# A new order table and one more product on constant tiles, in a decoder block whose instructions a planner puts in order

## The chip, the cores and the metric

One core of one Trainium2 chip. The metric is the time that the device takes for one execution, in microseconds; lower is better. The core's engines are named as in the profile: PE is TensorE (matrix products), PEld its loading of the stationary operand, DVE is VectorE, ACT is ScalarE, POOL is GpSimd, and SP is SyncE, whose queue here issues every transfer. PSUM is the memory that PE writes its results to.

## The reference, cut to what matters

A decoder block on 256 rows of 1024 numbers, in float32. Three mixers work on the normalised rows and are added with gates; then follows a gated channel mixer.

```python
h = rmsnorm(x, g_pre_mix)
z = h @ w_in
q_nsa, kv_nsa, g_nsa, qkv_ml, if_ml, o_ml, q_mem, g_merge = split(z)
...            # compressed, selected and windowed attention
y_nsa = gb[..., 0:1] * o_cmp + gb[..., 1:2] * o_slc + gb[..., 2:3] * o_win
...            # chunkwise mLSTM with a causal convolution of width 4
y_ml = sigmoid(o_ml) * h_ml
y_mem = memory_xattn(q_mem, mem, g_mem, w_mem_kv)   # keys and values: rmsnorm(mem) @ w_mem_kv
gm = sigmoid(g_merge)
y = gm[0] * (y_nsa @ w_proj_nsa) + gm[1] * (y_ml @ w_proj_ml) + gm[2] * (y_mem @ w_proj_mem)
x = x + rmsnorm(y @ w_out, g_post_mix)
h = rmsnorm(x, g_pre_ffn)
gu = h @ w_ffn_in
gate, up = gu[..., :2816], gu[..., 2816:]
x = x + rmsnorm((silu(gate) * up) @ w_ffn_down, g_post_ffn)
```

## The kernel before, in words

**The products.** Each large product is made of three products on rounded parts: an operand is split into a high part and a low part (`split`: ACT writes the high part `hi`, DVE subtracts it from the source and writes the low part `lo`), and PE adds high by high, high by low and low by high in PSUM. The weights come as 161 units of 128x1024 float32 (512 KB each). `fetch` issues the transfer of a unit into a tile `raw` on SP's queue; there are four buffers of `raw`. `parts` splits it into `whi` and `wlo` (four buffers each; for the first product of the feed-forward the parts are called `wq`). So a weight unit goes through SP, ACT, DVE and PE in that order, and each `raw` buffer comes free when its split is done.

**The stages.** First the keys and values of the memory tokens are made: `memt` holds the first inputs, `mh` and `ml` are the high and low parts of the memory tokens, and the results are in tiles `pd` and `pss` (PSUM tiles in general are called `pd`, `pss`, `ptn`, `pvn`, `sc`, `psm`, and so on). `mem_v` is the second of these products; its units are `whi`, `wlo` with `mh`, `ml`. Meanwhile the rows `x` are normalised (`xn`, `xt`, `rbc`) and split into `hh`; the memory's row norms come from `mn`. Then come the projections of `w_in`; four groups of attention in two halves each (`nsa_half`: `sc` is the scores on keys `kk` and queries `qs`, `mx` the masked maximum, `pp` and `pc` the exponentials, `ptn`, `pTh`, `pTl` their transposes and parts, `pvn` the product with the values, `ylo` and `yT` its sum), with the mLSTM's tasks put between the halves (`cx`, `cy` is the convolution, `vml` the values); then the merge. `w_out` is a product to two row halves of 128 rows (`tb` = 0, 1), each in two halves of 512 columns. Behind it `scaled` gives `xg` (the rows that go into the feed-forward), PE transposes `xg` into a PSUM tile that the trace calls `ptx`, and `split` writes it to `xc`, the operand of all of the feed-forward. The output of `ffn_down` goes out in pieces: per row half, columns 0 to 512, 512 to 768 and 768 to 1024 of a tile that the trace calls `z`, each one DVE instruction and one transfer.

**The order.** The kernel doesn't call engines directly. `Plan` records every operation with what it depends on; `schedule` then puts them in order with a list scheduler that keeps its own clock for every engine: of the operations that are ready on an engine it takes the one with the lowest `urge`. The urge is a rank, found by `choose` in some passes over the recorded operations, less a number from the table `EARLY` (operation's number: nanoseconds; a positive number makes the operation earlier). `lay_out` gives tiles their place, and `issue` emits the operations in that order; since it is one helper that calls the engines, all instructions of the kernel have the line L622 in the profile, and one goes by the tiles' names. All products, all splits and all transfers are in the hands of this order; each engine carries out its own instructions strictly one after the other, so an instruction that waits holds up those behind it on its engine.

**The start.** `warm_up(n)` records n products of a 128x128 tile of ones with itself into a PSUM tile `warm` that nobody reads. They stand in front of the first real product, and need no transfer. The table's numbers count recorded operations, so each product more in front moves the numbers of all later operations by one.

Of the kernel before, what the change touches and what calls it, by code (L numbers as in the profile page):

```python
# [167 lines left out]
class Plan:  # L168
# [363 lines left out]
    MATMUL, SLACK, PASSES = (-3.0, 0.0), (60.0, 130.0), 3  # L532

    EARLY = """
# [15 lines left out]
    """  # L550

    def choose(self):
# [73 lines left out]
def block_kernel(ctx, tc, order, xN, xT, memN, head, cst, vec, row, wg, w1, w2, W, out):  # L626
# [38 lines left out]
    def ps_v(shape, name="pv"):  # L665
        return psum.tile(shape, F32, tag="v", bufs=1, name=name)
# [95 lines left out]
    def warm_up(n):  # L762

        ps = ps_v([P, P], "warm")
        for _ in range(n):
            PE.matmul(ps, ones, ones, start=True, stop=True)
# [50 lines left out]
    part(1544, 2056)  # L817
    fetch(("mem_k", 2))
    part(2056, 3080)
    warm_up(8)  # L820
    warm = one.tile([P, 1], F32, name="warm")
    ACT.activation(warm, ones[:, 0:1], AF.Copy)
    kps = [ps_d([P, 2, S]) for _ in range(2)]
# [750 lines left out]
```

## Time and profile before

| | |
|---|---|
| runs | 524.69, 524.74, 526.28 us; median 524.74 |
| the profiled execution | 526.83 us; its span is 525.0 us, the granted clock 0.998 |
| PE busy | 516.7 us of the span, 3516 instructions in the profile |
| DVE, ACT, POOL busy | 412.9, 354.0, 6.2 us |
| transfers | 97.69 MB, 186 GB/s in the mean |

A row of the timeline reads: start in us, duration in us, engine, line, operation, output tile <- input tiles, shape, and how many instructions of one kind it groups (x4); in brackets the idle time of the engine ahead of it and what ended that. "SPq" is the issue of a transfer, not its flight. A product of float32 operands (`ones`) stands as two records. A row of windows gives, for a stretch from:to, its length and each engine's busy time with the number of instructions, then clock, share of the transfer engines and GB/s.

### The profile page before, as it was taken

The numbers are of one execution on the slowest core, as the hardware profiler recorded it, in microseconds if no ns is written. First come the engines' busy times: TensorE is split into PE (matmuls) and PEld (weight loads), VectorE is DVE, ScalarE is ACT, GpSimd is POOL, SyncE is SP. The second block draws the span as 40 slices with busy tenths as digits, with TensorE's granted clock in tenths as the row PEclk, the third lists the DMA queues.
The fourth block names the chain that finished last, engine by engine and source line by source line (L and its number), as shares of the span: only waits on it lengthen the run. The fifth ranks groups of instructions, "written<-read, shape, count | busy, mean of one in ns | idle before, by whom it ended". The sixth has DMA issues, their size and how long they took to land.

```text
span 525.0 us, 9545 instructions
## 1 busy us (share of the span) xinstructions
PE 516.7 (98%) x3516; PEld 475.6 (91%) x3516; DVE 412.9 (79%) x865; ACT 354.0 (67%) x724; POOL 6.2 (1%) x19
## 2 busy tenths in 40 slices
PE   8999999999999999999999999999999999999995
PEld 8999998989899999999999998788888888888884
DVE  5699898798989998988887888956776787664543
ACT  7777997577799887978995446554655665564531
POOL 0000000000000100000000000000000000000000
PEclk9999999999999999999999999999999999999999
DMA  8986546635343273264464766545555565566512
GB/s 316 416 310 265 182 140 209 214 122 199 122 152 131 86 275 122 85 199 161 162 201 160 215 223 213 193 131 190 180 187 194 186 201 184 196 196 199 187 61 81
DMA packets 28703, 97.69 MB, mean 186 GB/s; under 512 B 3312, under 2 KB 5232, under 8 KB 28400
## 3 DMA queue, kind: packets, MB, share of 16 engines
q1 hardware_dynamic: 28656, 97.07, 55.5%
q8 instruction: 28, 0.46, 0.3%
q14 instruction: 19, 0.16, 0.1%
HBM read 94.96 MB, written 1.05 MB: 183 GB/s over the span
## 4 chain that ended last, share of the span: by engine, by line
PE 91%; DMA 4%; DVE 3%; issue 1%; ACT 1%; DVEq 0%; ACTq 0%
PE pd L622 49%; PE pss L622 30%; PE pvn L622 2%; PE sc L622 2%; PE ptn L622 2%; DMA raw<-in_W 2%; DMA gp<-in_row 1%; DVE wlo L622 1%; DMA memt<-in_head 1%; PE ph L622 1%; DVE mrg L622 1%; PE psm L622 1%; PE pvm L622 1%; PE ptx L622 1%; PE pq L622 0%
## 5 line engine op out<-in xcount | busy, mean ns | idle before, releaser
L622 DVE TENSOR_TENSOR wlo<-raw,whi 128x1024 fp32r<-128x1024 f32 (+1 forms) x159 | 191.0, 1209 | 67.8 <-ACT whi L622 66.7
L622 ACT ACTIVATE whi<-raw 128x1024 fp32r<-128x1024 f32 (+1 forms) x159 | 165.9, 1052 | 110.1 <-PE pd L622 49.8
L622 PE MATMUL pd<-hh,whi 128*128 128x256 f32 x800 | 146.8, 280 | 0.0
L622 PEld LDWEIGHTS pd<-hh,whi 128*128 128x128 f32 x800 | 123.5, 188 | 0.2
L622 PE MATMUL pd<-hh,wlo 128*128 128x256 f32 x400 | 111.8, 280 | 0.0
L622 PEld LDWEIGHTS pd<-hh,wlo 128*128 128x128 f32 x400 | 75.2, 188 | 0.1
L622 PE MATMUL pss<-xc,whi 128*128 128x512 f32 x168 | 43.4, 393 | 0.0
L622 PE MATMUL pss<-whi,u 128*128 128x512 f32 x132 | 42.0, 390 | 0.0
L622 PEld LDWEIGHTS pss<-xc,whi 128*128 128x128 f32 x168 | 30.6, 188 | 5.3
L622 DVE CUSTOM_DVE_ANT_0 sc<-sc,msk 128x16 f32<-128x16 f32 (+2 forms) x96 | 27.3, 317 | 5.8 <-PE sc L622 3.7
L622 PE MATMUL pd<-xc,whi 128*128 128x512 f32 x120 | 31.8, 393 | 0.0
L622 PE MATMUL pd<-whi,hh 128*128 128x512 f32 x96 | 31.6, 397 | 0.0
L622 PEld LDWEIGHTS pss<-whi,u 128*128 128x128 f32 x132 | 24.8, 188 | 5.2
L622 ACT ACTIVATE pp<-sc,mx 128x128 f32<-128x128 f32 (+1 forms) x64 | 26.8, 434 | 0.5 <-DVE mx L622 0.3
L622 PE MATMUL pss<-wlo,u 128*128 128x512 f32 x66 | 25.7, 390 | 0.0
L622 PEld LDWEIGHTS pd<-xc,whi 128*128 128x128 f32 x120 | 22.2, 188 | 3.8
L622 PEld LDWEIGHTS pss<-xc,wlo 128*128 128x128 f32 x168 | 22.2, 188 | 1.7
L622 PE MATMUL pss<-xc,wlo 128*128 128x256 f32 x168 | 22.5, 278 | 0.0
L622 PEld LDWEIGHTS pd<-whi,hh 128*128 128x128 f32 x96 | 17.9, 188 | 3.2
L622 PE MATMUL pd<-wlo,hh 128*128 128x512 f32 x48 | 19.1, 397 | 0.0
L622 PE MATMUL sc<-kk,qs 128*128 128x272 f32 (+1 forms) x96 | 18.2, 291 | 0.0
L622 PEld LDWEIGHTS pd<-xc,wlo 128*128 128x128 f32 x120 | 15.8, 188 | 1.2
(328 smaller groups left out, 1040.4 us busy)
## 6 DMA issues: line engine op xcount, KB each, us to landing
raw<-in_W SPq DMA_DIRECT2D x161, 512.0 KB, 4.0
w<-in_w SPq DMA_DIRECT2D x2, 1024.0 KB, 7.9
xn<-in_xN SPq DMA_DIRECT2D x2, 512.0 KB, 9.1
mn<-in_memN SPq DMA_DIRECT2D x2, 512.0 KB, 7.9
xt<-in_xT SPq DMA_DIRECT2D x2, 512.0 KB, 8.7
kk<-kk SPq DMA_DIRECT2D x8, 128.0 KB, 3.2
x<-in_xN SPq DMA_DIRECT2D x2, 512.0 KB, 4.5
memt<-in_head SPq DMA_DIRECT2D x1, 512.0 KB, 7.4
```

What stands on the lines that cost most here:

```text
L622: op.ins_ = getattr(op.real, op.method)(*map(arg, op.a), **{k: arg(x) for k, x in op.kw.items()})
```

## The change

Two things. The table `EARLY` is replaced by another, with other operations and other numbers. And `warm_up(8)` becomes `warm_up(9)`.

```diff
     EARLY = """
-    2:182343850 3:30107850 4:28731400 5:28733050 6:1189450 7:1191000 145:12450 149:-600 151:1850 152:5000
...
-    4295:4700 4296:5700 4665:-6000 4673:-8200 5055:24850 5056:4350 5057:31850
+    2:267862150 3:43604600 4:40989750 5:40991450 6:1891200 50:2941700 146:9450 149:-2200 150:-1600 153:3350
...
+    4665:-550 5056:50900
     """
...
-    warm_up(8)
+    warm_up(9)
```

The computed operations stay the same, but for the one product. The order moves on every engine, in hundreds of places. Three of them follow, each as the engine's rows before and after; the numbers in names count tiles, and those of the two kernels don't match each other.

First ACT around the end of `w_out`, at about 331 to 336 us of the profile before. `whi_4597`, `whi_4615` and `whi_4636` (after: `whi_4602`, `whi_4625`, `whi_4644`) are splits of weight units, `xc` is the split of the transposed rows (of two tiles `ptx1`, which the trace calls `ptx`), `sq` a sum of squares. Before:

```order
L622 ACTIVATE wq_4585<-raw_4546 128x1024 [waits DMAHW2_49]
L622 ACTIVATE whi_4597<-raw_4566 128x1024 [waits DMAHW3_49,DVE_49,PE_49]
L622 ACTIVATE whi_4615<-raw_4581 128x1024 [waits DMAHW4_49,DVE_49,PE_49]
L622 ACTIVATE xc_4626<-ptx1_4609 128x4x128 [waits PE_49]
L622 ACTIVATE xc_4626<-ptx1_4618 128x4x128 [waits PE_49]
L622 ACTIVATE whi_4636<-raw_4599 128x1024 [waits DMAHW5_49,DVE_49]
L622 ACTIVATE sq_4643,ss_4521<-pd_4574 128x512 [waits PE_49,Activation_49]
```

And after:

```order
L622 ACTIVATE wq_4585<-raw_4555 128x1024 [waits DMAHW2_49]
L622 ACTIVATE whi_4602<-raw_4571 128x1024 [waits DMAHW3_49,DVE_49,PE_49]
L622 ACTIVATE xc_4619<-ptx1_4610 128x4x128 [waits PE_49]
L622 ACTIVATE whi_4625<-raw_4588 128x1024 [waits DMAHW4_49,DVE_49]
L622 ACTIVATE xc_4619<-ptx1_4617 128x4x128 [waits PE_49]
L622 ACTIVATE sq_4641,ss_4517<-pd_4575 128x512 [waits PE_49,Activation_49]
L622 ACTIVATE whi_4644<-raw_4605 128x1024 [waits DMAHW5_49,DVE_49]
```

The first `xc` now stands ahead of the second `whi`; the second `xc` stays behind it.

Second ACT at about 114 to 127 us, in the attention's second group. `ylo` ends one half of the group, `pp` and `pc` are exponentials of the next half's scores `sc`, `vml` the mLSTM's values. Before:

```order
L622 ACTIVATE ylo_1643<-pvn_1587 64x512 [waits PE_49]
L622 ACTIVATE whi_1655<-raw_1450 128x1024 [waits DMAHW4_49,PE_49]
L622 ACTIVATE whi_1669<-raw_1504 128x1024 [waits DMAHW5_49,PE_49]
L622 ACTIVATE vml_869<-pd_1552 128x4x128 [waits PE_49]
L622 ACTIVATE whi_1683<-raw_1572 128x1024 [waits DMAHW6_49,PE_49]
L622 ACTIVATE vml_869<-pd_1639 128x4x128 [waits PE_49]
L622 ACTIVATE whi_1706<-raw_1616 128x1024 [waits DMAHW7_49,Activation_49]
L622 ACTIVATE whi_1744<-raw_1685 128x1024 [waits DMAHW0_49,DVE_49,PE_49]
L622 ACTIVATE pp_1758,sm_1757<-sc_1695,mx_1738 128x256 [waits DVE_49]
```

And after:

```order
L622 ACTIVATE ylo_1645<-pvn_1587 64x512 [waits PE_49]
L622 ACTIVATE pc_1654,sm_1653<-sc_1627,mx_1638 128x16 [waits DVE_49]
L622 ACTIVATE pp_1658,sm_1653<-sc_1627,mx_1638 128x256
L622 ACTIVATE whi_1666<-raw_1451 128x1024 [waits DMAHW4_49,PE_49]
L622 ACTIVATE whi_1679<-raw_1504 128x1024 [waits DMAHW5_49,PE_49]
L622 ACTIVATE vml_803<-pd_1554 128x4x128 [waits PE_49]
L622 ACTIVATE whi_1698<-raw_1594 128x1024 [waits DMAHW6_49,PE_49,Activation_49]
L622 ACTIVATE vml_803<-pd_1648 128x4x128 [waits PE_49]
L622 ACTIVATE whi_1720<-raw_1629 128x1024 [waits DMAHW7_49,Activation_49]
L622 ACTIVATE whi_1753<-raw_1692 128x1024 [waits DMAHW0_49,DVE_49,PE_49]
L622 ACTIVATE pp_1658,sm_1653<-sc_1632,mx_1638 128x256 [waits DVE_49]
```

One pair of exponentials has moved from behind five `whi` and two `vml` to the place right behind `ylo`. PE makes the scores that they read ahead of it (three `sc` products among those of the first `pd` that `vml` reads), and one later `sc` product needs the exponential to be done.

Third DVE at the end. Before:

```order
L622 SCALAR_TENSOR_TENSOR z_6072<-z_6072,ss,x_2576 128x256 x2
L622 SCALAR_TENSOR_TENSOR z_6072<-pd,rf,go 128x512
L622 RECIPROCAL ss<-ss 128x1
L622 SCALAR_TENSOR_TENSOR z_6072<-z_6072,ss,x_2576 128x256 x2
L622 SCALAR_TENSOR_TENSOR z_6072<-z_6072,ss,x_2576 128x512
```

And after:

```order
L622 SCALAR_TENSOR_TENSOR z_6073<-pd,rf,go 128x512
L622 RECIPROCAL ss<-ss 128x1
L622 SCALAR_TENSOR_TENSOR z_6073<-z_6073,ss,x_2568 128x256
L622 SCALAR_TENSOR_TENSOR z_6073<-z_6073,ss,x_2568 128x512
L622 SCALAR_TENSOR_TENSOR z_6073<-z_6073,ss,x_2568 128x256
```

Of the last three pieces the one of 512 columns is now the second and no longer the last. On SP's queue, at the front, the transfer of the second half of `xt` now stands ahead of that of the second half of `mn`, the two loads `w1` (1 MB each, called `w` in the trace) stand behind two weight units more, and the eight copies within `kk` stand in two groups of four.

26 rows, old and new, of the table EARLY are left out of this document.

## Prediction

> **What bounds the kernel now.** I read the page first (busy shares, then the chain), then PE's waits, then the timeline of the few places where PE stands still.
>
> ```profile
> span 525.0 us, 9545 instructions
> PE 516.7 (98%) x3516; PEld 475.6 (91%) x3516; DVE 412.9 (79%) x865; ACT 354.0 (67%) x724; POOL 6.2 (1%) x19
> PE 91%; DMA 4%; DVE 3%; issue 1%; ACT 1%; DVEq 0%; ACTq 0%
> ```
>
> TensorE (PE) is busy for 516.7 of 525.0 us and carries 91% of the chain that ends last. So 8.3 us in all can be won by taking PE's idle time away, and part of that is the last output, which no order removes. The waits of PE on semaphores, from the view that groups them, are three:
>
> ```profile
> engine line waited for: us in total, times, longest us
> PE warm L622 <- POOL mhalf L622: 1.0, 1, 1.0
> PE pss L622 <- ACT xc L622: 0.7, 1, 0.7
> PE pd L622 <- ACT whi L622: 0.5, 1, 0.5
> ```
>
> The first is the start. The third is the first real product at 5.26, the second is at 335. The number and shape of the real products stay as they are, so the sum has a term for the start, one for 335, one for the last output, and a question mark wherever the new order might make a fourth wait.
>
> The profiled execution took 526.83 us, its span is 525.0, so 1.83 lie around the span. It is 2.09 above the median of the runs (524.74; 524.69 and 526.28 the others). A change of 0.3% is 1.57 us; less than that a measurement of this kernel can't tell from none. Faster means below 523.17, slower above 526.31.
>
> **Part 1, the ninth constant product.** The timeline of the first microseconds, and PE's rows around 10.5 us:
>
> ```profile
> 0.99 3.78 PE L622 MATMUL warm<-ones 128*128 128x128 f32 x16 [0.99 <-POOL mhalf L622]
> 4.57 0.63 ACT L622 ACTIVATE whi<-memt 128x512 fp32r<-128x512 f32 x1 [1.93 <-DMA memt<-in_head]
> 5.26 1.23 PE L622 MATMUL pd<-mh,whi 128*128 128x256 f32 x4 [0.49 <-ACT whi L622]
> 9.69 1.03 PE L622 MATMUL pd<-mh,wlo 128*128 128x256 f32 x4
> 10.55 0.65 PE L622 MATMUL pd<-mh,whi 128*128 128x256 f32 x4
> 11.03 0.62 PE L622 MATMUL pd<-ml,whi 128*128 128x256 f32 x4
> ```
>
> The eight products of `ones` are 16 records, 3.78 us, so 0.24 each. They end at 4.77; ACT makes the first `whi` from 4.57 to 5.20 because its data land only then; PE idles 0.49. One product more is two records, 0.47 us: it ends at 5.24, inside the idle time, and delays nothing (bounds 0 and +0.1). It only replaces idle by busy.
>
> What that is worth hangs on the clock. Four products begun at 9.69 are followed 0.86 us later (0.215 each); four begun at 10.55 are followed after 0.48 (0.12 each). So PE runs at half rate until about 10.5 us. From 5.26 on, 5.3 us of half rate cost at most half of that, 2.6 us. [...] This is not paid out in full, since the products would then catch up with their data. The tightest place I found is the product with the low part of the second V unit:
>
> ```profile
> 25.22 3.50 DVE L622 TENSOR_TENSOR wlo<-raw,whi 128x1024 fp32r<-128x1024 f32 x3
> 27.86 0.39 PE L622 MATMUL pss<-wlo,mh 128*128 128x512 f32 x1
> 28.08 0.39 PE L622 MATMUL pss<-whi,ml 128*128 128x512 f32 x1
> ```
>
> VectorE's (DVE's) first of three is done a third of 3.50 after 25.22, about 26.4; PE uses it at 27.86. So 1.4 us of head start are usable. The bounds of the term are 0 and −1.4.
>
> Which end? The runs before fall into two groups, 524.7 (two) and 526.3 to 526.8 (one, and the profiled one), 1.5 to 2.1 apart. That is the size of an early or a late lift of the clock, and I know no other thing here of that size that differs between executions of one program. I read the profiled execution as a late one and the median as an early one. Against the median, then, the ninth product changes nothing in the likeliest case: 0. Against the profiled execution it may be the whole distance.
>
> [...]
>
> **Part 2, the place at 335 us.** Here the gate of the feed-forward (`pss<-wq,xc`) waits for `xc`, the split of the transposed `xg`. ACT, DVE, PE and the chain:
>
> ```profile
> 330.89 1.07 ACT L622 ACTIVATE whi<-raw 128x1024 fp32r<-128x1024 f32 x1 [1.31 <-DMA raw<-in_W]
> 333.39 1.06 ACT L622 ACTIVATE whi<-raw 128x1024 fp32r<-128x1024 f32 x1 [1.43 <-DMA raw<-in_W]
> 334.35 1.07 ACT L622 ACTIVATE xc<-ptx 128x512 fp32r<-128x512 f32 x2
> 332.88 1.22 DVE L622 TENSOR_TENSOR wlo<-raw,whi 128x1024 fp32r<-128x1024 f32 x1
> 334.96 1.29 DVE L622 TENSOR_TENSOR xc<-ptx,xc 128x512 fp32r<-128x512 f32 x2 [0.86 <-ACT xc L622]
> 332.28 0.60 PE L622 MATMUL ptx<-cs,xg 128*128 128x128 f32 x4
> 333.88 0.40 PE L622 MATMUL pd<-whi,yh 128*128 128x512 f32 x1
> 334.98 1.47 PE L622 MATMUL pss<-wq,xc 128*128 128x512 f32 x4 [0.71 <-ACT xc L622]
> 328.13 5.15 DMA raw<-in_W
> ```
>
> The last transposes are issued at 332.28, so their output is there by 332.9 at the latest. ACT idles 1.43 us then, because the next instruction in its queue is a `whi` whose `raw` is in flight until 333.28, 5.15 us after its issue (raw units land in 4.0 in the median). Only after that `whi` come the two `xc`, at 334.35, and PE begins the gate at 334.98. Products of 512 columns follow each other after some 0.23 us (27.86, 28.08 above, 0.22 by rounding), so unhindered the gate would begin at 334.11: 0.87 lost. The four rows `x4` take 1.47 where three steps of 0.23 and one last 0.40 make 1.09: 0.38 more. Together 1.25.
>
> In the new order one `xc` stands ahead of that `whi`. It needs 1.07/2 ≈ 0.55 us, runs at about 332.4 to 332.9 in ACT's idle time, and costs the `whi` nothing (ACT is free again before 333.39). DVE makes the low part after its `wlo`, which ends at 334.10: 334.1 + 0.65 = 334.75. PE's first two products need the high part only and start at 334.11; the third is due at 334.57 and waits some 0.14. The second half of the transposes stands five products earlier on PE after the gate's first ones, about 337.4, where `xg` of that half, by the same steps as before, is ready near 337.65: 0.23 more. What is left of 1.25 is 0.37: −0.9. Bounds: −1.25 if both leftovers vanish, and +0.3 if the late `raw` still holds the second `xc` (it stands behind the same `whi` as before) and the transposes wait longer than I think. I take −0.9, since the cause, an idle ACT beside ready data, is taken away and the leftovers are worked out one by one.
>
> **Part 3, the last output.**
>
> ```profile
> 520.49 1.54 DVE L622 SCALAR_TENSOR_TENSOR z<-z,ss,x 128x256 f32<-128x256 f32 x3
> 521.00 1.39 SPq L622 DMA_DIRECT2D out<-z  x3
> DMA to landing us min/median/max: 1.8/2.0/2.2
> ```
>
> The three pieces (256, 256, 512 columns) become 256, 512, 256. DVE's time for them stays 1.54; the last transfer has half the size. The spread of landings, 1.8 to 2.2, is all that size can be worth: 0 to −0.4; I take −0.1, since neighbouring landings mostly differ by that much.
>
> **Part 4, where a fourth wait could come.** Between 112 and 123 us the new order puts a first group of score products (`sc`), their masked maxima on DVE and their exponentials on ACT (`pc`, `pp`, right behind `ylo`) ten microseconds earlier; three more score products follow at about 122 and one of them waits for that exponential.
>
> ```profile
> 116.19 0.60 ACT L622 ACTIVATE ylo<-pvn 64x512 f32<-64x512 f32 x1 [0.93 <-PE pvn L622]
> 117.57 1.06 ACT L622 ACTIVATE whi<-raw 128x1024 fp32r<-128x1024 f32 x1 [0.79 <-PE pd L622]
> 126.21 0.47 ACT L622 ACTIVATE pp<-sc,mx 128x256 f32<-128x256 f32 x1
> 126.91 0.47 ACT L622 ACTIVATE pp<-sc,mx 128x256 f32<-128x256 f32 x1
> 121.67 0.90 PE L622 MATMUL sc<-kk,qs 128*128 128x272 f32 x6
> 122.42 0.40 PE L622 MATMUL pd<-hh,whi 128*128 128x256 f32 x2
> 121.22 0.69 DVE L622 TENSOR_TENSOR vml<-pd,vml 128x512 fp32r<-128x512 f32 x1
> 112.50:125.00 12.50, 12.50 (x77) 11.11 (x76) 11.93 (x24) 8.05 (x13) 0.22 (x2) 1.00 0.41 137
> ```
>
> ACT idles 0.79 from 116.79 to 117.57. One pair of exponentials takes 0.70 (126.21 to 126.91): it fits, 4.9 us ahead of its use at 122.4. DVE has less room, 11.93 of 12.50. The maxima of the pair cost it some 0.6; one `yT` of 0.4 leaves the stretch. `vml` ends at 121.91 before, 0.5 ahead of its user at 122.42; with +0.2 it still does. I cost this at 0, with +0.3 as upper bound.
>
> The eight copies of `kk` on SP's queue stand closer together behind two weight units more. They are read late:
>
> ```profile
> L622 SPq DMA_DIRECT2D kk<-kk x8: 596/602/1408, 73.9 to 88.7; - x8
> L622 PE MATMUL sc<-kk,qs x14: 281/288/292, 100.3 to 122.3; 128*128 128x272 f32 x12, 128*128 128x256 f32 x2
> ```
>
> Eleven microseconds lie between the last issue and the first score: 0. At the front of that queue the second half of `xt` now goes ahead of the second half of `mn`, which helps PE's next inputs, and the two `w1` loads go behind two weight units more.
>
> ```profile
> 34.15 0.90 SPq L622 DMA_DIRECT2D w<-in_w  x2
> 44.43 1.06 ACT L622 ACTIVATE w1s<-w 128x1024 fp32r<-128x1024 f32 x1
> ```
>
> They are first read 10.3 us after their issue began: 0 while two units fit into that, a wait of the size of the one at 335 if they don't. The other moves go with their producers. I price all of these at 0, bounds −0.3 and +1.3 (another place like 335).
>
> **The sum.** 526.83 − 0 (clock as in this execution) − 0.9 − 0.1 + 0 = 525.8 in a late execution; taken to the median, 524.74 − 1.0 = 523.7.
>
> **Rivals.**
> A (the forecast): 335 eased, last output smaller, clock as in the runs before: 523.7, own range 523.1 to 525.0 by the bounds of parts 2 to 4.
> B: the ninth product closes the gap and the clock lifts earlier than in the median run too: 524.74 − 1.4 − 1.0 = 522.3. [...] Against it: two of the three runs are likely early already without it.
> C: the change doesn't do what it says. The wait at 335 moves on to the next late `raw` or to the transposes, and the clock stays: 524.6. For it: each `whi` there waits on its transfer (1.31, then 1.43).
> D, slower: the early score products at 122 us. If their maxima are pushed behind DVE's work and the exponential comes only where it stood, 126.2 to 127.4, PE stands still from 122.42 for up to 5.0 us: 523.7 + 5.0 = 528.7. It decides from a delay of 2.6 us on, when the exponential ends after 125.0. Against it: 4.9 us of cover.
>
> **How the numbers follow.** A 0.52, B 0.27, C 0.11, D 0.10 (D stands for such a wait anywhere in the reordered stretches). Faster by over 0.3% comes from B (0.27) and the low edge of A (0.06): 0.33. Slower from D: 0.10. Within 0.3%: the rest of A and C, 0.57. The range leaves out D and the lowest part of B (gains past the cover, 0.07): 521.9 to 525.7.
>
> **What the profile after would show.** Part 1: the idle before the first real product at 5.26 falls from 0.49 to under 0.1, and PE's groups of four are 0.48 apart before 10.5 us (B), or not (A). Part 2: PE's wait for ACT `xc` falls from 0.7 to 0.3 or less, and an `xc` stands in ACT's row before the `whi` at 333. Part 3: the last landing follows its issue by 1.8 or so, not 2.0. Part 4: no wait of PE for ACT `pp` or DVE `vml` near 122. I would be wrong if a new row with more than 1 us stood in PE's waits, or if PE's busy time differed from 516.7 by over 1 us, which would mean another rate of products.

## The result, and the profile after

The change makes the kernel slower: 528.3 us in the median of six runs (528.21 to 528.60), beside 524.72 for the kernel before in the same session (six runs, 524.27 to 526.28). The ratio is 1.0066, interval 1.0056 to 1.0076, some 3.5 us. The forecast was 523.7, its range ended at 525.7.

The head of the page of the changed kernel (profiled execution 528.22 us), the engines of its chain, and PE's waits:

```profile
span 526.4 us, 9543 instructions
PE 517.1 (98%) x3518; PEld 476.0 (90%) x3518; DVE 414.4 (79%) x865; ACT 353.6 (67%) x723; POOL 6.2 (1%) x19
PE 93%; DMA 3%; DVE 2%; ACT 1%; issue 1%; SPq 0%; DVEq 0%; ACTq 0%
PE warm L622 <- POOL mhalf L622: 1.0, 1, 1.0
PE pd L622 <- ACT whi L622: 0.9, 2, 0.7
```

These views look better than those of before: PE is busy as long as it was (517.1 for 516.7), and the wait for `xc` is gone. None of them holds 3.5 us. The loss lies in two places that neither the busy time nor the waits show: the distance from one product to the next, and the last transfer.

**The distance between products.** The same 20 us of the merge, before and after, in the view of windows, PE's column first (busy time and number of matmul records):

```profile
280.00:300.00 20.00, 20.00 (x179) 1.00 0.65 203
...
280.00:300.00 20.00, 20.00 (x172) 1.00 0.57 190
```

PE is busy throughout in both, the granted clock is 1.00 in both, but the new order gets 172 records done where the old one had 179. PE's timeline there, first before, then after:

```profile
290.24 0.39 PE L622 MATMUL pss<-ymlt,whi 128*128 128x256 f32 x2
290.58 0.39 PE L622 MATMUL pss<-ymlt,whi 128*128 128x256 f32 x2
290.92 0.39 PE L622 MATMUL pss<-ymlt,whi 128*128 128x256 f32 x2
```

```profile
290.23 0.40 PE L622 MATMUL pss<-ymlt,whi 128*128 128x256 f32 x2
290.59 0.40 PE L622 MATMUL pss<-ymlt,whi 128*128 128x256 f32 x2
290.94 0.40 PE L622 MATMUL pss<-ymlt,whi 128*128 128x256 f32 x2
```

Between two such rows lie three products (the single one with `wlo` isn't shown). Read the starts, not the durations: 0.34 for three before, 0.355 after. Taken from the start times of all products of 256 columns that follow one of 256 columns from 10.5 us on, there are two distances and little between them: 113.4 ns and 117.8 ns, in either kernel. I call them the fast and the slow pitch. Before, 580 of some 2050 stand at the slow pitch, after 1048 of some 2020; at 4.4 ns each the difference of 468 is 2.1 us. Between 262 and 323 us alone (the merge and the start of `w_out`) there are 38 before and 343 after, almost all of the latter without a break: 1.3 us. Products of 512 columns separate less clearly (227 and 232 in the mean), with 235 and 237 at the slow one: no difference.

**The last output.** The transfers of the output after (before: 1.8, 2.0, 2.2), then the transfers from 520 us on, by queue and by tile (columns: packets, MB, share; KB each, median us to landing), and the issue of the last three:

```profile
DMA to landing us min/median/max: 1.8/2.0/3.2
q14 instruction: 1, 0.01, 0.4%
out<-z SPq DMA_DIRECT2D x2, 128.0 KB, 2.5
521.22 1.47 SPq L622 DMA_DIRECT2D out<-z  x3
```

One of the last three lands 3.2 us after its issue. Behind its last data packet and ahead of its last small one (4 bytes, 524.48) stands a packet of another kind, on a queue that carries instructions: 8 KB at 524.07 us, 0.4 us long. Fifteen of the sixteen parts of the last transfer are reported done by 524.43, the sixteenth at 525.47. From the last product's start to the end of the span it is 7.66 us after, 6.47 before, where the nearest fetch of that queue comes at 507.7.

**The three places of the forecast.** The start of PE after:

```profile
0.99 3.92 PE L622 MATMUL warm<-ones 128*128 128x128 f32 x18 [0.99 <-POOL mhalf L622]
5.16 0.74 PE L622 MATMUL pd<-mh,whi 128*128 128x256 f32 x4 [0.25 <-ACT whi L622]
5.74 0.62 PE L622 MATMUL pd<-ml,whi 128*128 128x256 f32 x4
8.83 0.74 PE L622 MATMUL pd<-mh,whi 128*128 128x256 f32 x4 [0.66 <-ACT whi L622]
```

The groups of four are 0.46 apart from 5.74 on, so the clock is up early: the trace's record of the granted clock, 1.00, begins at 4.46 us, in the profile before at 10.55. At 8.83 PE then stands still for 0.66, since ACT has waited 0.89 us for the weight unit's data, until 8.15.

ACT and PE at the place where the gate begins, and ACT at 115 us:

```profile
331.80 1.06 ACT L622 ACTIVATE whi<-raw 128x1024 fp32r<-128x1024 f32 x1 [0.36 <-DMA raw<-in_W]
333.48 0.60 ACT L622 ACTIVATE xc<-ptx 128x512 fp32r<-128x512 f32 x1 [0.62 <-PE ptx L622]
333.98 1.05 ACT L622 ACTIVATE whi<-raw 128x1024 fp32r<-128x1024 f32 x1
335.11 0.40 PE L622 MATMUL pd<-whi,yh 128*128 128x512 f32 x1
335.34 2.01 PE L622 MATMUL pss<-wq,xc 128*128 128x512 f32 x8
```

```profile
115.39 0.59 ACT L622 ACTIVATE ylo<-pvn 64x512 f32<-64x512 f32 x1 [0.54 <-PE pvn L622]
116.26 0.46 ACT L622 ACTIVATE pp<-sc,mx 128x256 f32<-128x256 f32 x1
117.23 1.06 ACT L622 ACTIVATE whi<-raw 128x1024 fp32r<-128x1024 f32 x1 [0.41 <-PE pd L622]
```

The first `xc` stands ahead of the `whi`, and the gate follows the product before it after 0.23: no wait. The exponential `pp` sits in ACT's gap behind `ylo`, and PE has no wait at 122.

### The profile page after: what moved, and what is told of

The parts are those of the page before. It is cut to its first block, busy times and chain, and to the rows that moved or that the text cites. A ratio compares the mean times of both kernels' runs of the same rounds, so it can differ in the third digit from the quotient of the medians.

```text
span 526.4 us, 9543 instructions
## 1 busy us (share of the span) xinstructions
PE 517.1 (98%) x3518; PEld 476.0 (90%) x3518; DVE 414.4 (79%) x865; ACT 353.6 (67%) x723; POOL 6.2 (1%) x19
## 3 DMA queue, kind: packets, MB, share of 16 engines
HBM read 94.96 MB, written 1.05 MB: 182 GB/s over the span
## 4 chain that ended last, share of the span: by engine, by line
PE 93%; DMA 3%; DVE 2%; ACT 1%; issue 1%; SPq 0%; DVEq 0%; ACTq 0%
PE pd L622 50%; PE pss L622 31%; DMA raw<-in_W 3%; PE pvn L622 2%; PE sc L622 2%; PE ptn L622 2%; DVE wlo L622 1%; PE ph L622 1%; PE ptx L622 1%; PE psm L622 1%; PE pvm L622 1%; ACT whi L622 1%; PE pn L622 1%; PE pq L622 0%; DVE xt L622 0%
## 5 line engine op out<-in xcount | busy, mean ns | idle before, releaser
L622 DVE TENSOR_TENSOR pTl<-ptn,pTh 128x512 fp32r<-128x512 f32 x24 | 16.0, 682 | 2.5 <-ACT pTh L622 2.5
```

The source lines that it names most:

```text
L622: op.ins_ = getattr(op.real, op.method)(*map(arg, op.a), **{k: arg(x) for k, x in op.kw.items()})
```

## The experiments

The diffs below are shortened to what they do. The theories were: the table or the product (E1, E2); the fetch of DVE's instructions (E3, E5, E12, E13, E15, E16); the slow pitch as a state that something sets anew (E3, E4, E6, E7, E8, E10); the clock's price (E1, E11); the wait at 335 (E9, E14). "Slow" below is the number of products of 256 columns at the slow pitch in the profiled execution, counted as above; "tail" is the time from the last product's start to the end of the span. Where two kernels have the same order on PE, their products can be set beside each other one by one; "early" and "late" then say by how much a product of the one starts before or behind the same product of the other.

**E1, the old table with nine constant products.**

```diff
-    warm_up(8)
+    warm_up(9)      # and the old table's numbers from 145 on raised by one
```

> The old order with nine constant products. The traces of before and after differ at the start: with nine products the real ones run at 114 ns from 5.2 us on (in the profile of before only from 10.5 on). Theory A (the ninth product alone makes the clock rise early in every run, and the loss lies in the new order): 523.0 to 524.7, with all runs within 0.4 us, and the first real product at full rate. Rival (the ninth product itself brings the loss, by what comes after an early clock): 526.5 or more.

Measured: 524.74 (523.73 to 526.01), ratio 0.9995 (0.9985 to 1.0005); slow 583, tail 6.47. The product alone changes nothing. The order on PE is that of before, and so this profile (span 522.8) tells why the profiled execution of before was 2.1 us above its median: E1's products are 1.9 us early at 10.5 us, 1.5 from 41 to 322 us, 2.1 from 342 us to the end, and the later steps lie nowhere else. So 1.5 is the later clock of that execution, and 0.6 a longer wait at 335.

**E2, the new table with eight.** The same edit the other way round, on the changed kernel.

> The new order with eight constant products. Theory A: the new order is slower by itself, and without the ninth product some runs have the late clock as well: a median of 528.3 to 530.2, runs in two groups. Rival (the ninth product brings the loss): below 526.

Measured: 528.59 (527.75 to 528.97), 1.0066 (1.0052 to 1.0079); slow 1148, tail 7.6, the fetch at 524.9. The whole loss is the table's.

**E3, twelve small DVE instructions in the changed kernel.** Ahead of an operation at 487 us, into a new tile that lies ahead of most others and moves them (by 32 bytes per partition, as I take it).

```diff
+    if op.i == 4907:
+        pad = first_pool.tile([P, 2], F32)
+        for _ in range(12):
+            DVE.tensor_scalar(pad, ones[:, 0:2], 1.0, 0.0, op0=ALU.mult, op1=ALU.add)
```

> The changed kernel with 12 small DVE instructions more (128x2, at 487 us, where DVE idles). In the trace of after, an 8 KB instruction fetch at 524.07 sits among the last output's packets, whose completion comes in 3.2 us instead of 2.0. Theory: it is DVE's fetch, which the new order, with four DVE queue instructions less, has pushed from 507.7 behind DVE's last instruction; 12 instructions more bring it forward again: 527.2, the last landing 2.0 us after its issue. Rival (the fetch is of another engine, or the last landing is late for another reason): 528.3, landing still 3.2.

Measured: 526.09 (525.41 to 527.25), 1.0024 (1.0014 to 1.0033): 2.2 us better than without them. The fetch comes at 506.3, the largest landing is 2.2, the tail 6.59. But the merge also went at the fast pitch (64 slow products there for 343; product by product 1.2 us are gained there). Two things had changed at once, so E5 and E6 take them apart.

**E4, one short product in the changed kernel.** At 265.4 us, ahead of an operation (3075) where the slow stretch begins, a product of 64 columns whose result the next one overwrites.

```diff
+    if op.i == 3075:
+        matmul(out[:, 0:64], lhs, rhs[:, 0:64], start=True, stop=True)
```

> The changed kernel with one short product more (64 columns) in front of the merge's first product at 265.4 us. In the trace of after, products of 256 columns follow each other after 117.8 ns from 264.9 to 306.8 (338 in a row), in before after 113.3 for nearly all of that stage. Theory (a rhythm of loads and products that holds itself once it is entered, and that any break can end): the merge goes back to 113.3 and the time falls by 338 x 4.5 ns = 1.5 us, to 526.8. Rival (the slow pitch comes from what lies beside it, tiles' places or transfers): 528.3 or 0.1 more, pitch still 117.8. A break that doesn't end the rhythm would look like the rival in this run.

Measured: 528.06, 1.0059 (1.0046 to 1.0072). Behind it the pitch is fast up to the transposes, which begin at 268.62, then slow again to 307: a miss for the time, but the pitch can be changed by what is issued.

**E5, E3's instructions with their tile behind all others,** so that every address stays.

```diff
-        pad = first_pool.tile([P, 2], F32)
+        pad = last_pool.tile([P, 2], F32)
```

> As the kernel with 12 small DVE instructions, but their target lies behind all other tiles, so that no tile's place moves (there it had moved most tiles by 32 bytes, and the merge ran at 113.3 ns as well). Theory: the end alone is mended: last PE start to the end of the span 6.6 us instead of 7.7, 527.2 us; the merge stays at 117.8 ns. Rival (the instructions themselves end the slow pitch): 525.8 to 526.1.

Measured: 527.71 (527.01 to 528.19), 1.0047 (1.0032 to 1.0062); tail 6.59. The output's landings and the last transfers:

```profile
DMA to landing us min/median/max: 1.8/2.0/2.2
out<-z SPq DMA_DIRECT2D x2, 128.0 KB, 2.0
...
280.00:300.00 20.00, 20.00 (x172) 1.00 0.57 189
```

The fetch has moved to 508.7 and the tail is 1.07 shorter, although DVE has more to do. The merge is as slow as before the edit (x172). Set beside the changed kernel, product by product, nothing differs by over 0.04 from 61 to 322 us. Between 327 and 336 us E5's profiled execution loses 1.0, behind a `whi` whose transfer came late, and that hides the gain in this one execution; in the medians the gain is 0.6 to 1.0 us (527.71 for 528.3; by the ratios 1.0047 for 1.0066). The intervals still overlap a little; the tail is the firmer proof.

**E6, 32 bytes.** A tile that nobody uses, ahead of the large ones, in the changed kernel.

```diff
+    first_pool.tile([P, 8], F32)
```

> The changed kernel with an unused tile of 32 bytes, which moves the places of all large tiles by 32 bytes, and nothing else. Theory (where the slow rhythm of products is entered depends on tiles' places as well as on the order): the merge runs at 113.3 ns for the most part, 526.8; the late end stays (landing 3.1). Rival (places don't matter; the merge became fast by the 12 instructions or by chance): 528.3, merge at 117.8.

Measured: 526.71 (526.38 to 528.70), 1.0041 (1.0025 to 1.0058); slow 644; the merge has the records of before again, and the last output's landings are shorter:

```profile
280.00:300.00 20.00, 20.00 (x179) 1.00 0.61 192
...
DMA to landing us min/median/max: 1.8/2.1/2.4
```

The order is the changed kernel's on every engine. Product by product, E6 gains 1.2 us between 262 and 323 us, and 343 − 67 slow products at 4.4 ns are 1.2. It had lost 0.5 at the start (its clock rose later), and gains 0.1 at 364 and 0.8 in the tail: −1.6 together, as measured. The 0.8 was luck. The fetch comes where it did, 5.38 us behind the last product's start for 5.37, but the transfer's last small packet got ahead of it (5.38, in the changed kernel 5.78), and the sixteenth part was 0.23 late and not 1.04. So the 526.8 that was forecast from the pitch alone was met in part by the tail, and the runs lie in two groups (five from 526.4 to 526.9, two from 528.4 to 528.7). What stands is the 1.2 in the merge: the order alone does not set the pitch; the places of the tiles have a part in it.

**E7, three short products.** As in E4, ahead of three operations of the merge.

> The changed kernel with three short products of 64 columns, in front of the products that begin new sums at 265.4, 272.7 and 280.3 us. With one at 265.4 the pitch was 113 ns until the transposes at 269, and 117.8 from there to 307. Theory (transposes enter the rhythm, a short product ends it; no transposes come after 269.8): slow from 269 to 272.7 only, some 30 products instead of 338: 528.3 - 1.3 = 527.0. Rival (the first break ended the rhythm by chance; the slow pitch of the merge comes from elsewhere): 528.2, some 300 products at 117.8.

Measured: 527.99 (526.80 to 529.07), 1.0055 (1.0039 to 1.0071); slow 967: a miss for the time (527.0 was forecast). The first two ended the slow pitch. The third, the row with 64 columns in PE's timeline, began it:

```profile
279.34 0.28 PE L625 MATMUL pss<-ynh,wlo 128*128 128x256 f32 x1
279.45 0.28 PE L625 MATMUL pss<-ynh,whi 128*128 128x256 f32 x1
279.57 0.28 PE L625 MATMUL pss<-ynl,whi 128*128 128x256 f32 x1
279.68 0.28 PE L625 MATMUL pss<-ynh,wlo 128*128 128x256 f32 x1
279.79 0.19 PE L624 MATMUL pss<-ynh,whi 128*128 128x64 f32 x1
280.02 0.28 PE L625 MATMUL pss<-ynl,whi 128*128 128x256 f32 x1
280.14 0.28 PE L625 MATMUL pss<-ynh,wlo 128*128 128x256 f32 x1
280.26 0.28 PE L625 MATMUL pss<-ynh,whi 128*128 128x256 f32 x1
280.38 0.28 PE L625 MATMUL pss<-ynl,whi 128*128 128x256 f32 x1
```

Ahead of it 0.34 for three steps, behind it 0.36, and so it stays to 306 us.

**E8, eight short products in the kernel before.** Each within a slow stretch there.

> The kernel before with eight short products (64 columns), each in front of a product that begins a new sum within a slow stretch of its trace (at 54.7, 102.7, 150.2, 177.7, 197.7, 206.2, 216.9 and 236.8 us). Theory (a short product ends the rhythm, here too): some 280 of its 600 slow products become fast, -1.27 us, against 8 x 0.06 for the short ones: 524.7 - 0.8 = 523.9. Rival (the break doesn't hold, or what comes next enters it again): 524.7 + 0.5 = 525.2.

Measured: 524.95 (524.54 to 525.81), 0.9997 (0.9987 to 1.0008); slow 477: a miss (523.9). Half of them ended their stretch, but product by product E8 loses 0.5 between 52 and 250 us all the same, so the short products cost more than the faster pitch gained. Of the twelve short products of E4, E7 and E8 seven led from slow to fast, four left slow as it was, and one led from fast to slow: they draw anew, they don't cure.

**E9, the old table with one move by hand.** Only ACT's first `xc` is put ahead of the `whi` that waits for its data.

```diff
+    late = next(op for op in order if op.i == 3786)   # ACT's whi at 333
+    order.remove(late)
+    order.insert(1 + next(k for k, op in enumerate(order) if op.i == 3682), late)   # behind the first xc
```

> The kernel before, with one change on ACT alone: the first split xc at 335 us stands ahead of the whi that waits for its transfer, as in the new order. The prediction's part 2 (0.9 us won where the wait at 335 costs 1.25): 523.9, PE's wait for xc at 335 gone or below 0.3. Rival (the wait in that place changes from run to run with the transfers, 1.4 us in the profile of before and 0.7 to 0.8 in two later ones of the same order, and the next late thing takes its place): 524.5 to 525.0.

Measured: 524.29 (523.77 to 524.97), ratio 0.999 (0.9981 to 0.9998), 0.5 us below the kernel before (0.1 to 1.0 by the interval) and the lowest median of all the kernels here. ACT and PE:

```profile
331.18 0.60 ACT L625 ACTIVATE xc<-ptx 128x512 fp32r<-128x512 f32 x1 [1.44 <-PE ptx L625]
331.68 1.05 ACT L625 ACTIVATE whi<-raw 128x1024 fp32r<-128x1024 f32 x1
332.81 0.40 PE L625 MATMUL pd<-whi,yh 128*128 128x512 f32 x1
333.04 4.15 PE L625 MATMUL pss<-wq,xc 128*128 128x512 f32 x17
```

Against the profiled execution of before, the products gain 1.2 at this place and nothing behind it. But the same gain comes without the move. E11 below has the old order here, with both `xc` behind the `whi`, and yet its gate doesn't wait, because the transfer came in time:

```profile
331.63 1.06 ACT L622 ACTIVATE whi<-raw 128x1024 fp32r<-128x1024 f32 x1 [0.54 <-DMA raw<-in_W]
332.59 1.06 ACT L622 ACTIVATE xc<-ptx 128x512 fp32r<-128x512 f32 x2
333.38 0.40 PE L622 MATMUL pd<-whi,yh 128*128 128x512 f32 x1
333.62 2.59 PE L622 MATMUL pss<-wq,xc 128*128 128x512 f32 x10
```

What the place costs can be counted as the time of nine steps, from the last product ahead of the gate, over 0.233 each. That is 1.24 in the profiled execution of before, but 0.11 to 0.68 in the eight other profiles of the old order without the move (E1, E8, E10, E11, E12, E13, E15, E16), 0.37 in the median; 0.06 in E9, and 0.38 in E14, which has the move as well. So the profile before shows this place at its worst, and the 0.5 of the medians is about all that it usually holds.

**E10, the 32 bytes in the kernel before.**

> The kernel before with an unused tile of 32 bytes, which moves all large tiles by 32 bytes, and no other change. In the new order this alone took the number of slow products (117.8 ns) from some 1170 to 679 and the time from 528.3 to 526.7. Theory (places draw anew where the slow rhythm is entered; 600 slow products is a good draw of the old order): between 600 and 1000 slow products, 524.7 plus 4.4 ns for each above 600, 525 to 526.5. Rival (shifted places are better for any order): fewer than 500, 524.2 or less.

Measured: 524.80, 0.9997 (0.9988 to 1.0005); slow 493. Neither more slow products, as the theory had it, nor a gain: the old order has few slow products to lose.

**E11, the old table with four constant products,** meant to make the clock rise late.

> The old order with four constant products instead of eight; PE then idles some 2.2 us in front of the first real product. Theory (an idle stretch of about 0.5 us or more in the first 5 us puts the rise of the clock off to 10.5 us, as in the profile of before; most runs of the kernel before have it earlier): every run late, 526.3 to 527. Rival (the rise of the clock doesn't hang on that idle time): 524.7.

Measured: 525.30 (524.74 to 526.31), 1.0007 (0.9998 to 1.0016): a miss, 526.3 or more was forecast.

```profile
0.99 2.07 PE L622 MATMUL warm<-ones 128*128 128x128 f32 x8 [0.99 <-POOL mhalf L622]
5.04 1.22 PE L622 MATMUL pd<-mh,whi 128*128 128x256 f32 x4 [1.97 <-ACT whi L622]
```

The groups of four stay 0.85 apart until 9.5 us. Beside E1's, its products are 1.46 late up to 26 us, 1.05 from 28 to 324 us, but only 0.4 from 344 on: by then the split of `xc` is ready, and E11 has next to no wait there. So a late clock cost 0.4 here (0.6 by the ratios of E1 and E11), since part of it is waited away later. In the profiled execution of before, as late as E11 to within 0.5 us up to 331 us, it was not: there the transfer at 335 was late too.

**E12, E13, E15, E16, the fetch in the kernel before.** 116, 120, 121 and 123 small DVE instructions, spread ahead of fourteen operations from 4750 to 4951, are to bring a fetch of the old order among the packets of the last output. The 128 entries from fetch to fetch that the first expectation goes by are read from the traces: after, nine of the 19 fetches of 8 KB come when 63, 189, 323, 440, 577, 699, 828, 962 and 1087 of DVE's 1090 entries have begun, 117 to 137 apart and 128 in the mean (before, 118 to 140 and 127, the last with 1079 of 1094 begun); the other ten fit the entries of ACT (71 to 831 in seven, 127 apart in the mean) and of SP (80, 208 and 335).

```diff
+    for _ in range(pads.get(op.i, 0)):   # 116, 120, 121 or 123 in all
+        DVE.tensor_scalar(pad, ones[:, 0:2], 1.0, 0.0, op0=ALU.mult, op1=ALU.add)
```

> The kernel before with 116 small DVE instructions more (128x2, eight or nine ahead of each of 14 weight splits between 462 and 496 us, where DVE idles), with their target behind all other tiles. DVE's instruction fetch lay 15 DVE entries before the end of its list (507.7 us); fetches come every 128, so 116 more put one 3 entries before the end, where the new order has it. Theory: the fetch comes at about 522 to 524 us, the last landing takes 3.1 us instead of 2.0, and the time rises by 1.0 to 525.8. Rival (the late fetch does no harm by itself, or it isn't DVE's): no fetch after 510 and 524.7, or a fetch there and 524.7.

> As with 116 small DVE instructions, but 120. With 116 the last fetch of DVE came at 471.3 us, at its entry 1082 of 1210, and the next would have come with entry 1210, past the end; with 120 the list has 1214 entries, and the fetch falls some 4 before the end. Theory: a fetch at 522 to 525 us, the last landing 3 us after its issue, the time 0.5 to 1.0 above the 524.6 of 116. Rival (a fetch there does no harm in the old order): 524.6.

> As with 120 small DVE instructions, but 121. With 120 the fetch came at 524.9 us, behind the last landing. One entry earlier it should come at about 522 to 524, as in the new order. Theory: then the last landing takes some 3 us instead of 2.0, and the span ends 7.4 to 7.7 us after the last product instead of 6.5; time 525.5 to 526. Rival: landing 2.0, 524.7.

> As before with 123, two entries earlier again. Theory: the fetch comes ahead of the last output's packets or with their first ones, and the harm is smaller or none: 6.5 to 6.9 us from the last product to the end. Rival: as with 121.

Measured, all misses: with 116 no further fetch came (524.63; 0.9997, 0.9986 to 1.0009). With 120 it came at 524.9, with 121 at 524.5, with 123 at 524.4, each time behind the last landing and behind the end of the span (523.8, 523.3, 524.1). The tails are 6.47, 6.48 and 6.76; in the last the output lands 2.0 us after its issue as ever, so the 0.28 more are not the fetch's. The times, 525.37 (1.0010, 1.0001 to 1.0019), 526.00 (1.0037, 1.0024 to 1.0051) and 526.17 (1.0032, 1.0020 to 1.0044), are mostly the instructions' own: at 495 us PE waits for a `wlo` behind them and loses 0.5, 0.8 and 1.2. None of the four had a fetch among the output's packets, so they test nothing about it. That the fetch delays the output is shown in the new order (E5, E3), and untested in the old one.

**E14, E9's move and the 32 bytes.**

> The old order with the one xc moved and all large tiles 32 bytes further. Each was tried alone: the move gave 0.5 us, the places took the slow products from 604 to 524. Theory (the two add up): 524.3 - 80 x 4.4 ns = 523.9. Rival (the places' draw doesn't hold with the move): 524.3 or more.

Measured: 524.59 (523.90 to 526.28), 0.9998 (0.9989 to 1.0008); slow 493. Neither gain shows.

## Why the prediction was wrong, step by step

**Part 1 (the ninth product, 0): right.** E1 shows 0, and the reading of the spread held in the main: of the 2.1 us of the profiled execution 1.5 were a late clock and 0.6 the wait at 335. B's sign, groups 0.46 apart well before 10.5, did appear, but the other profiles with eight products have it too, so it is no gain over the median. The price of rival B was too high: E11's late clock cost 0.4 to 0.6 and not 1.4. The cap by the data at 27.86 was well placed: E1's lead over the profile before falls from 1.9 to 1.5 there, and over E11 from 1.46 to 1.05. What the price lacked was the place at 333, where E1 loses 0.6 more of its lead over E11. The time at which the clock rises differs between executions with eight products: late in the profile of before (0.48 apart only from 10.55 on), and products 1.0 to 1.7 us earlier by 21 us in the profiles of E8, E9, E10 and E12, which have eight as well. That the idle time ahead of the first product decides it was B's assumption. No run shows it as the cause, though the late ones are those with the most of it: the groups are some 0.46 apart from 5.60 and 6.85 on with none there (E10, E1), from 5.74 and 6.58 with 0.25 and 0.19 (the changed kernel, E9), and from 10.55 and 10.13 with 0.49 and 1.97 (before, E11).

**Part 2 (335, −0.9): right in kind, too large.** The wait is gone after, by the move that was named. But it was sized on an execution in which the place cost 1.24; in the eight other profiles of the old order it cost 0.37 in the median. The move by itself was worth 0.5 in E9's median (0.1 to 1.0), and nothing clear in E14. A slip in the sum changes little: by its own times the third product waits 334.75 − 334.57 = 0.18, not 0.14.

**Part 3 (the last output, −0.1): wrong in sign, +1.2.** The sum looked at the transfer's size. What ended it was a fetch of instructions in its way, and its bounds (0 to −0.4) had no room for that. E5 puts 1.07 of it on the fetch. Even without the fetch the smaller last piece won nothing: E5's tail is 6.59, that of before 6.47.

**Part 4 (the place at 122, 0): right.** No wait arose, so rival D, though it lies at 528.7 beside the measured 528.3, was not what happened; its number is near by chance. A's own range, 523.1 to 525.0, holds the bounds of parts 2 and 3 only; with those of part 4 (−0.3 and +1.3) it would be 522.8 to 526.3, still below the 528.3.

**The step that failed is the sentence ahead of the parts:** the products' number and shape stay, so the sum needs no term for them. They cost 2.1 us more, at the same number, shape, clock and busy time. The closing condition did name "another rate of products", but it looked for it in PE's busy time. That grew by 0.4 only: the rows above last longer with the step (0.40 for 0.39), so PE counts as busy through it. With 2.1 for the pitch and 1.2 for the tail, 3.3 of 3.6 us are found; the early waits of the new order (0.66 at 8.83) and the 0.5 won at 335 nearly cancel, and the rest lies within what runs differ by.

**What stays open** is why a product falls into the one pitch or the other. In the profiles it holds over hundreds of products, comes back at the same places in executions of one order (E5, E2 and the changed kernel agree to 0.04 us from 61 to 322 us), and changed at transposes (E4, 268.62 us), at short products (E7, 279.79 us) and with the places of tiles (E6). Only the merge's 1.2 us were taken away by an experiment (E6, and E3); that the other 0.9 is the same is read from the distances.

## What to carry to other kernels

When PE is busy 98% of the time, compare the starts of like products, not busy time and waits: 4% between two products is 2 us here and shows in neither view. A planner with one rate per shape can't see this, so an order that promises less than about 0.5% has to be timed (the 2.1 us of the pitch are 0.4% here), and a small shift of the tiles is a cheap second draw (1.2 us in E6, nothing in E10). A wait found in one profile is worth the whole only in executions like it: look at the same place in several before pricing it. Here E9's single move gave half of what was forecast, and still beat a table with hundreds.

## What the runs showed of the hardware that was not expected

- Products of 128x256 in fp32r at full clock stood at two steady distances, 113.4 and 117.8 ns, and kept one over hundreds of products; 32 bytes in the tiles' places changed it in one stretch (343 slow products to 67) with the order unchanged.
- An 8 KB fetch of instructions ahead of the last output's last small packet delayed one of sixteen parts by 0.94 to 1.04 us (the changed kernel, E2, E4, E7); with that packet ahead of it, in E6, the delay was 0.23. Twelve more instructions on DVE moved the fetch by 15 us, so it is DVE's. DVE, whose last operation ends at 522.25, did not wait for the one at 524.07, and the output's landing did.
- An early clock, 1.46 us ahead at 23 us and 1.05 at 41 us in E1 against E11, was worth 0.4 at the end.
